# Splitting the first turned block of activations between ScalarE and VectorE, in a pooled-attention decoder trunk on Trainium2

## The chip, the cores and the metric

The kernel runs on one core of one Trainium2 chip. The metric is the device time of one execution in microseconds (us). The profile names the engines PE (TensorE matmuls), PEld (TensorE weight loads, which overlap PE), DVE (VectorE), ACT (ScalarE), POOL (GpSimd) and SP (SyncE, which here issues most of the DMAs).

## The reference, cut to what matters

Two layers work on an input `x` of 512 tokens by 1024 channels in float32. Layer 0 mixes the tokens by a causal multi-scale pooling, layer 1 by a differential attention; each is followed by a SwiGLU feed-forward network with 2816 hidden rows.

```python
for i in range(DEPTH):                                   # DEPTH = 2
    h = _multiscale_pool(x, ...) if i == 0 else _diff_attention(x, ...)
    x = _layernorm(ALPHA * x + h, ln_mix_g[i], ln_mix_b[i])
    x = _layernorm(ALPHA * x + _swiglu(x, w_gate[i], w_up[i], w_down[i]), ln_ffn_g[i], ln_ffn_b[i])
```

The change lies where layer 0 passes from the pooling mixer's layer norm (number 0) to the first gate and up products of its feed-forward network.

## The kernel before, in words

**Numbers in two parts.** Every float32 matrix product is made of three matmuls on a rounded high part and a low part (the rest): high by high, high by low, low by high (`mm3`, lines 147 to 151, so the three matmuls show as L149, L150 and L151). `split` (lines 116 to 124) makes the parts: ScalarE copies the high part (L123), then VectorE, or GpSimd where `low` says so, subtracts it from the source (L124). Weights arrive by SP's DMAs into five buffers `raw` (L111). `ready(upto)` splits the weight rows up to a number into `w<c>h` and `w<c>l`; w2 to w5 are the weights of the first gate, the first up, the second gate and the second up product.

**Tokens.** The 512 tokens are four blocks of 128. `res` holds them with tokens on the partitions. For each block s the mixer's matmuls (`mixed`, into PSUM banks `mix`) are added to `res` (`residual`, L183), the sums for mean and variance are taken (`stat`, L190), mean and variance are put together (`spread_of`, L196 to L199; the power of -0.5 runs on GpSimd, L199), and `norm` (L208) writes the normalised block. `summed` is `residual` and `stat` together.

**Turns.** The feed-forward network needs the block with channels on the partitions and in two parts, in `xt`. `transposed(0, s)` makes eight 128x128 transposes on TensorE into two PSUM banks `pt` of four each (L235). `turned(0, s)` then goes bank by bank: four ScalarE activations apply gain and bias (L249) into an SBUF tile `y`, and `split` makes `xt`'s two parts out of `y`, 512 columns at a time. Blocks 0 and 1 are turned before the feed-forward network starts; blocks 2 and 3 in its midst, at the places that the argument `late` names.

**Order.** All instructions stand in an order written by hand (`manual_schedule`): each engine runs its own in the order in which the program issues them, and waits on semaphores for the others. At the start of the network `ffn` makes three pairs of a gate and an up product (`early = 3`; f counts the pairs, i is 0 for gate and 1 for up), first for tokens 0 to 255 (`lo = 0`), then for tokens 256 to 511. A product is 24 matmuls of 256 columns: for each of the eight k blocks the three of `mm3`. Behind the product (f, i) of the first half stands `late[f, i]`, if there is one, then `advance`, which splits the next weights (g_4 and g_5, L610 and L613). `lines`, a small table for layer 1, is written to DRAM by a DMA that ScalarE issues (L487 to L491).

Of the kernel before, what the change touches and what calls it, by code (L numbers as in the profile page):

```python
# [12 lines left out]
F32 = mybir.dt.float32  # L13
F32R = mybir.dt.float32r
BF16 = mybir.dt.bfloat16
AF = mybir.ActivationFunctionType
ALU = mybir.AluOpType

P = 128
# [4 lines left out]
KB = D // P  # L24
SB = S // P
FB = FF // P
HEADS = 8
# [10 lines left out]
LINE = 640  # L38
NEAR = 512
# [15 lines left out]
def trunk(ctx, tc, x, wall, pscale, lam_p, subln, table, lng, lnb, band, first, onehot, out):  # L55
    nc = tc.nc

    keep = ctx.enter_context(tc.tile_pool(name="keep", bufs=1))
# [3 lines left out]
    def bank(name):  # L62
        return ps.tile([P, 512], F32, tag="bank", name=name)


    xt = keep.tile([P, 2, 2, KB, 256], F32R, name="xt")
# [49 lines left out]
    def split(dst_h, dst_l, src, scale=1.0, low=None):  # L116
        if scale != 1.0:
            nc.scalar.mul(dst_h, src, scale)
            nc.vector.scalar_tensor_tensor(
                dst_l, src, scale, dst_h.bitcast(F32), op0=ALU.mult, op1=ALU.subtract  # L120
            )
        else:
            nc.scalar.copy(dst_h, src)  # L123
            (low or nc.vector).tensor_tensor(dst_l, src, dst_h.bitcast(F32), op=ALU.subtract)  # L124

    def ready(upto, low=None):
        while divided[0] < min(upto, total):
            c = divided[0]
            fetch(c + RAWS)
            h, l = weight_pair(f"w{c}")  # L130
            raw = raws.pop(c)
            if c in by_dma:
                nc.scalar.copy(h, raw)
                nc.scalar.mul(l, raw, -1.0)
                nc.gpsimd.dma_start(
                    out=l, in_=wall[rows_of_wall[c]].bitcast(F32R), accum_op=ALU.add
                )
            else:
                split(h, l, raw, low=low)
            parts[c] = (h, l)  # L140
            divided[0] += 1
# [18 lines left out]
    gT = keep.tile([P, 2 * DEPTH, KB], F32, name="gT")  # L160
    bT = keep.tile([P, 2 * DEPTH, KB], F32, name="bT")

    def x_at(k, lo, hi):

        if hi - lo > 256:
            return tuple(xt[:, :, i, k, :] for i in range(2))
        a = lo // 256
        return tuple(xt[:, a, i, k, lo - 256 * a : hi - 256 * a] for i in range(2))

    def wide(acc, lo, hi):  # L170
        return acc.rearrange("p (a b) -> p a b", a=2) if hi - lo > 256 else acc[:, lo:hi]
# [9 lines left out]
    def residual(s, d, acc, scale=ALPHA):  # L181
        z = res[:, s, d * 512 : (d + 1) * 512]
        nc.vector.scalar_tensor_tensor(z, z, scale, acc, op0=ALU.mult, op1=ALU.add)  # L183
# [3 lines left out]
    def stat(n, s, d):  # L187
        if (n, s) not in stats:
            stats[n, s] = keep.tile([P, 2, 6], F32, tag="st", name=f"st{n}_{s}", bufs=4)
        nc.vector.bn_stats(stats[n, s][:, d, :], res[:, s, d * 512 : (d + 1) * 512])  # L190
# [3 lines left out]
    def spread_of(n, s):  # L194
        mv = keep.tile([P, 2], F32, tag="mv", name=f"mv{n}_{s}", bufs=2)
        nc.vector.bn_aggr(mv, stats.pop((n, s)))  # L196
        rs = keep.tile([P, 1], F32, tag="rs", name=f"rs{n}_{s}", bufs=2)
        nc.vector.tensor_scalar(rs, mv[:, 1:2], scalar1=EPS, scalar2=None, op0=ALU.add)  # L198
        nc.gpsimd.tensor_tensor(rs, rs, mhalf, op=ALU.pow)  # L199
        scales[n, s] = (mv, rs)  # L200

    def norm(n, s, done=None):
        if (n, s) not in scales:
            spread_of(n, s)
        mv, rs = scales.pop((n, s))
        z = res[:, s, :]
        if not done:
            nc.vector.tensor_scalar(  # L208
                z, z, scalar1=mv[:, 0:1], scalar2=rs, op0=ALU.subtract, op1=ALU.mult
            )  # L210
            return
        gb = gbs[n]
        halves = [slice(d * 512, (d + 1) * 512) for d in range(2)]
        for c in halves:
            nc.vector.scalar_tensor_tensor(
                z[:, c], z[:, c], mv[:, 0:1], gb[:, 0, c], op0=ALU.subtract, op1=ALU.mult
            )
        for c in halves:
            nc.vector.scalar_tensor_tensor(
                z[:, c], z[:, c], rs, gb[:, 1, c], op0=ALU.mult, op1=ALU.add  # L220
            )
            done(s, c)
# [7 lines left out]
    turns = {}  # L230
# [10 lines left out]
    def turned(n, s, kept=None):  # L241
        for i, pt in enumerate(turns.pop((n, s))):
            if kept:
                y = kept[i][:, :, s % 2 * P : (s % 2 + 1) * P]
            else:
                y = keep.tile([P, 4, P], F32, tag="y", name=f"y{n}_{s}_{i}", bufs=2)
            for k in range(4):
                kk = 4 * i + k
                nc.scalar.activation(  # L249
                    y[:, k, :],  # L250
                    pt[:, k * P : (k + 1) * P],
                    AF.Identity,
                    bias=bT[:, n, kk : kk + 1],
                    scale=gT[:, n, kk : kk + 1],
                )
            o = (s % 2) * P
            split(*(xt[:, s // 2, j, 4 * i : 4 * i + 4, o : o + P] for j in range(2)), y)

    def turn(n, s):
        transposed(n, s)  # L260
        turned(n, s)
# [21 lines left out]
    with tc.tile_pool(name="pool", bufs=1) as pp:  # L283
# [108 lines left out]
        def split_pooled(half, *groups):  # L392
            for g in groups:
                c = slice(half * 256, (half + 1) * 256)
                split(
                    ph[:, 2 * g : 2 * g + 2, c],
                    pl[:, 2 * g : 2 * g + 2, c],
                    made[half, g].rearrange("p (k t) -> p k t", k=2),
                )

        mixes = {}
# [19 lines left out]
        def summed(s, *ds):  # L421
            for d in ds:
                residual(s, d, mixes[s][d])
                stat(0, s, d)
# [25 lines left out]
        mixed(2, 0)  # L450
        summed(0, 1)
        spread_of(0, 0)
        split_pooled(1, 2, 3)
        norm(0, 0)
        tbh = pp.tile([33, HEADS], F32R, name="tbh")
        tbl = pp.tile([33, HEADS], F32R, name="tbl")
        ohr = pp.tile([33, NEAR], F32R, name="ohr")
        split(tbh, tbl, tb)
        nc.scalar.copy(ohr, oh_)
        transposed(0, 0)  # L460
# [4 lines left out]
        mm(lines_bank[:HEADS], tbl, ohr, start=False, stop=True)  # L465
        summed(1, 0, 1)
        spread_of(0, 1)
        summed(2, 0)
        norm(0, 1)
        transposed(0, 1)  # L470
        mixed(3, 1)
        turned(0, 0)
        summed(2, 1)
        spread_of(0, 2)
        turned(0, 1)
        ready(4)
        summed(3, 0, 1)
        norm(0, 2)
        spread_of(0, 3)
        ready(5)  # L480
        norm(0, 3)
        ready(6)

        line = pp.tile([HEADS, LINE], F32, name="line")
        far = pp.tile([HEADS, 1], F32, name="far")
        nc.gpsimd.memset(line[:, NEAR:], 0.0)
        nc.scalar.copy(far, lines_bank[:HEADS, NEAR - 1 :])  # L487
        nc.scalar.activation(
            line[:, :NEAR], lines_bank[:HEADS], AF.Identity, bias=far, scale=-1.0
# [14 lines left out]
    def ffn(layer, late):  # L504
        n = 2 * layer + 1
# [4 lines left out]
        with tc.tile_pool(name=f"ffn{layer}", bufs=1) as fp:  # L510
# [111 lines left out]
                if upto > len(chunks):  # L622
                    prepare(upto - len(chunks), upto - len(chunks))

            def product(acc, j, lo, hi):
                h, l = halves[j]
                for k in range(KB):
                    mm3(
                        wide(acc, lo, hi),
                        (h[:, k * P : (k + 1) * P], l[:, k * P : (k + 1) * P]),  # L630
                        x_at(k, lo, hi),
                        k == 0,
                        k == KB - 1,
                    )
# [155 lines left out]
            accs = [(bank(f"g{layer}_{f}"), bank(f"u{layer}_{f}")) for f in range(early)]  # L790
# [3 lines left out]
            for lo in (0, 256):  # L794
                for f in range(early):
                    for i in range(2):
                        product(accs[f][i], 2 * f + i, lo, lo + 256)
                        if not lo and (f, i) in late:
                            late[f, i]()
                        if not lo:  # L800
                            advance(2 * early, True)
                    if lo:
                        advance(2 * f + 6)
                        gated(order[f], *accs[f])
                        affine(n - 1, f)
                        catch_up()
                        if f < 2:
                            weight_sums()
                            next(sums)
                        if f == 1:  # L810
                            behind.append(sum_hidden(0))
# [83 lines left out]
            f = early  # L895
# [40 lines left out]
            banks = {}  # L936
            done = store if final else None
            for p in DOWN:
# [5 lines left out]
                accs = banks[{"P1": "P1", "Q5": "Q5", "Q3": "Q5", "P2": "P2"}.get(p, "P1")]  # L944
                together = len(PAIRS) - (tail if p == "Q4" else 0)
                for i in range(together):
                    j = j0 + i
# [463 lines left out]
    def later(n, s):  # L1411
        return lambda: turn(n, s)

    ffn(0, {(0, 1): later(0, 2), (1, 0): later(0, 3)})
    attention()
    ffn(1, {(0, 1): later(2, 3)})

# [107 lines left out]
```

## Time and profile before

| | |
|---|---|
| Time, median of 3 runs (lowest, highest) | 948.29 us (948.05 to 949.07) |
| Time of the profiled execution | 948.47 us |
| Its span from the first to the last instruction | 946.7 us |
| Mean granted TensorE clock | 0.997 |
| Busy: PE, PEld, DVE, ACT, POOL | 931.2, 829.9, 787.3, 513.8, 126.5 us |

The span leaves 1.8 us of the profiled execution outside the trace. A line of a timeline gives the start in us, the time of it, the engine, the line of the kernel, the operation, the tiles it writes and reads, and in brackets how long the engine had stood idle before and what ended that. Rows of one kind in a row are merged (x4). On DVE and PE the next instruction starts a little before the one ahead of it has ended, so that the distance between starts is shorter than the durations.

### The profile page before, as it was taken

The page shows a single profiled execution, that of the slowest core. Times are in us where ns is not written, and L with a number is a line of the kernel's source. Part 1 is how long each engine was busy: PE and PEld are TensorE (multiplying, and loading weights), DVE is VectorE, ACT ScalarE, POOL GpSimd, SP SyncE. Part 2 cuts the span into 40 slices and gives each one's busy share as a digit, 9 for nine tenths or more (in the row PEclk, how much of TensorE's full clock was granted, in tenths as well). Part 3 has the DMA queues.
Part 4 walks back from the last instruction along what each step waited for, and adds up shares of the span by engine and source line. Part 5 has one row for each costly group of instructions (what it writes and reads, how often), then busy time and mean ns, then how long its engine had stood idle before and what let it go on. Part 6 is the DMA issues. An engine that isn't in the chain of part 4 may idle for free.

```text
span 946.7 us, 14942 instructions
## 1 busy us (share of the span) xinstructions
PE 931.2 (98%) x5712; PEld 829.9 (88%) x5712; DVE 787.3 (83%) x1158; ACT 513.8 (54%) x819; POOL 126.5 (13%) x152
## 2 busy tenths in 40 slices
PE   9999999999999999999999999999999999999996
PEld 8898899999988878887888878998899999988884
DVE  8858989999988489968887886789779999987778
ACT  6752344555564357666878753843345554664450
POOL 4120211110001201101111100211111110001101
PEclk9999999999999999999999999999999999999998
DMA  8386988986868996875666522396988886878952
GB/s 240 125 267 225 327 265 273 269 251 215 256 209 270 350 314 189 211 196 150 155 160 138 141 90 81 118 325 214 270 252 248 251 278 202 258 248 276 349 169 90
DMA packets 86038, 211.11 MB, mean 223 GB/s; under 512 B 15140, under 2 KB 26660, under 8 KB 85966
## 3 DMA queue, kind: packets, MB, share of 16 engines
q1 hardware_dynamic: 43420, 117.16, 37.5%
q0 software_dynamic: 18768, 58.20, 24.8%
q10 hardware_dynamic: 23778, 34.78, 10.2%
q8 instruction: 45, 0.74, 0.3%
q14 instruction: 27, 0.22, 0.1%
HBM read 173.40 MB, written 36.72 MB: 222 GB/s over the span
## 4 chain that ended last, share of the span: by engine, by line
PE 82%; DVE 9%; ACT 3%; DMA 3%; issue 2%; POOL 0%; DVEq 0%; ACTq 0%; POOLq 0%
PE A L861 17%; PE P L928 9%; PE C L861 9%; PE B L861 4%; PE Q L928 3%; PE g L151 3%; PE u L149 3%; PE u L150 3%; PE u L151 3%; PE g L149 3%; PE g L150 3%; PE va L1076 2%; PE s L1142 2%; DMA r<-tsum 1%; DMA r<-in_wall 1%
## 5 line engine op out<-in xcount | busy, mean ns | idle before, releaser
L607 DVE TENSOR_TENSOR raw<-raw,raw 128x1024 f32<-128x1024 f32 x56 | 68.3, 1219 | 0.5
L123 ACT CAST xs<-hid 128x512 fp32r<-128x512 f32 (+1 forms) x60 | 34.7, 582 | 24.4 <-DVE hid L775 24.4
L124 DVE TENSOR_TENSOR xs<-hid,xs 128x512 fp32r<-128x512 f32 (+1 forms) x60 | 38.5, 643 | 7.8 <-ACT xs L123 7.8
L1158 ACT ACTIVATE p<-p,mn 128x128 f32<-128x128 f32 (+3 forms) x64 | 35.2, 552 | 12.4 <-DVE mn L1153 12.4
L249 ACT ACTIVATE y<-pt,bT,gT 128x128 f32<-128x128 f32 x80 | 30.1, 456 | 19.4 <-PE pt L235 19.4
L706 POOL DMA_DIRECT2D b<-in_wall x20 | 14.0, 706 | 170.8 <-DMA tsum<-b 70.4
L767 POOL DMA_DIRECT2D xs<-ssum x24 | 17.4, 726 | 141.6 <-PE Q L928 68.5
L199 POOL TENSOR_TENSOR rs<-rs,mhalf 128x1 f32<-128x1 f32 x16 | 12.5, 784 | 152.0 <-DVE rs L198 112.6
L639 DVE TENSOR_TENSOR hid<-sg,u 128x512 f32<-128x512 f32 x16 | 11.0, 687 | 26.1 <-PE u L151 14.1
L743 ACT CAST v<-u 128x512 fp32r<-128x512 f32 x22 | 13.6, 620 | 27.7 <-DVE u L741 27.7
L706 POOL DMA_DIRECT2D hid<-in_wall x24 | 18.7, 823 | 74.4 <-DMA tsum<-hid 43.9
L1153 DVE CUSTOM_DVE_ANT_0 p<-s,bias 128x128 f32<-128x128 f32 (+3 forms) x64 | 28.0, 485 | 0.7 <-PE s L1142 0.7
L124 DVE TENSOR_TENSOR xt<-y,xt 128x512 fp32r<-128x512 f32 x20 | 13.6, 690 | 12.1 <-ACT xt L123 12.1
L190 DVE BATCH_NORM_STATS2 st<-res 128x6 f32<-128x512 f32 x32 | 22.2, 695 | 1.1
L887 ACT ACTIVATE sg<-sg 128x512 f32<-128x512 f32 x14 | 8.9, 633 | 25.7 <-DVE sg L880 25.7
L707 POOL DMA_DIRECT2D hid<-in_wall x12 | 14.8, 1233 | 58.5 <-DMA hid<-in_wall 51.1
L655 ACT CAST xs<-hid 128x1024 fp32r<-128x1024 f32 x8 | 8.4, 1051 | 26.0 <-DVE hid L672 11.6
L1142 PE MATMUL s<-heads 64*128 64x256 f32 (+2 forms) x168 | 20.0, 353 | 1.1 <-ACT heads L123 0.8
L1142 PEld LDWEIGHTS s<-heads 64*128 64x128 f32 x168 | 14.1, 185 | 5.2 <-issue 1.0
L1172 DVE SCALAR_TENSOR_TENSOR p<-p,sm,p 128x128 f32<-128x128 f32 (+3 forms) x32 | 17.7, 552 | 1.1
L876 DVE TENSOR_TENSOR hid<-C,hid 128x512 f32<-128x512 f32 x14 | 9.7, 691 | 10.4 <-PE C L861 8.8
L872 ACT COPY hid<-C 128x512 f32<-128x512 f32 x14 | 8.2, 589 | 18.5 <-PE C L861 18.5
(1187 smaller groups left out, 3666.3 us busy)
## 6 DMA issues: line engine op xcount, KB each, us to landing
raw<-in_wall SPq DMA_DIRECT2D x122, 512.0 KB, 4.8
r<-tsum SPq DMA_DIRECT2D x40, 512.0 KB, 4.5
hid<-in_wall POOLq DMA_DIRECT2D x36, 512.0 KB, 7.4
b<-in_wall POOLq DMA_DIRECT2D x30, 512.0 KB, 6.0
r<-in_wall SPq DMA_DIRECT2D x30, 512.0 KB, 4.6
tsum<-hid ACTq DMA_DIRECT2D x24, 512.0 KB, 5.6
ssum<-v ACTq DMA_DIRECT2D x22, 512.0 KB, 4.3
tsum<-b ACTq DMA_DIRECT2D x20, 512.0 KB, 4.9
```

What stands on the lines that cost most here:

```text
L123: nc.scalar.copy(dst_h, src)
L124: (low or nc.vector).tensor_tensor(dst_l, src, dst_h.bitcast(F32), op=ALU.subtract)
L149: nc.tensor.matmul(acc, ah, bh, start=start, stop=False)
L150: nc.tensor.matmul(acc, ah, bl, start=False, stop=False)
L151: nc.tensor.matmul(acc, al, bh, start=False, stop=stop)
L249: nc.scalar.activation(y[:, k, :], pt[:, k * P : (k + 1) * P], AF.Identity, bias=bT[:, n, kk : kk + 1], scale=gT[:, n, kk : kk + 1],)
L607: tt(t, raws[pair[0]], raws[pair[1]], op=ALU.add)
L706: nc.gpsimd.dma_start(out=t[:, j], in_=src[:, j])
L861: nc.tensor.matmul(o, w[:, c], x[:, kk, :], start=p in ("P1", "Q5", "P2") and f + kk + e == 0, stop=p in ("Q4", "Q3", "P2") and (f, kk, e) ...
L928: nc.tensor.matmul(accs[s], x[:, k, r], y[:, c], start=first and k == 0 and e == 0, stop=last and k == m - 1 and e == 2, skip_group_check= ...
L1142: nc.tensor.matmul(accs[c][:, :wide], a[r, qs], b[r, :wide], start=i == 0, stop=i == 2)
L1158: nc.scalar.activation(p, p, AF.Exp, bias=mn[:, q, c : c + 1], scale=-1.0, accum_out=sm[:, q, c : c + 1],)
```

## The change

Six things are changed, all in the stretch from the mixer's end to the first half of the first three product pairs.

1. `turned(0, 1)` becomes `turned_apart(0, 1)`: ScalarE's eight activations read the PSUM banks and write the rounded high parts straight into `xt`; VectorE's eight `tensor_scalar` read the same banks and write `y`; then VectorE subtracts twice.
2. The first gate product (layer 0, f = i = 0, tokens 0 to 255) takes, for each half of the k blocks, four high by high, four low weight by high, then four high weight by low.
3. `ready(4)`, which splits w3, stands ahead of `split_pooled(1, 2, 3)` and `norm(0, 0)`, and its subtraction is on GpSimd. `ready(5)` stands behind the turn of block 1, `ready(6)` behind `spread_of(0, 2)`.
4. Of `summed(2, 0)` the `stat` is moved behind the turn and `ready(5)`; `norm(0, 2)` comes ahead of `summed(3, 0, 1)`.
5. The tiles `line` and `far` and the GpSimd memset of `line` are moved ahead, behind `norm(0, 0)`.
6. Blocks 2 and 3 are turned behind the products (1, 0) and (1, 1) instead of (0, 1) and (1, 0).

```diff
+    def turned_apart(n, s):
+        o = (s % 2) * P
+        banks = turns.pop((n, s))
+        ys = []
+        for i, pt in enumerate(banks):
+            y = keep.tile([P, 4, P], F32, tag="y", name=f"y{n}_{s}_{i}", bufs=2)
+            for k in range(4):
+                kk = 4 * i + k
+                bias, scale = bT[:, n, kk : kk + 1], gT[:, n, kk : kk + 1]
+                a = pt[:, k * P : (k + 1) * P]
+                nc.scalar.activation(
+                    xt[:, s // 2, 0, kk, o : o + P], a, AF.Identity, bias=bias, scale=scale
+                )
+                nc.vector.tensor_scalar(
+                    y[:, k, :], a, scalar1=scale, scalar2=bias, op0=ALU.mult, op1=ALU.add
+                )
+            ys.append(y)
+        for i, y in enumerate(ys):
+            h, l = (xt[:, s // 2, j, 4 * i : 4 * i + 4, o : o + P] for j in range(2))
+            nc.vector.tensor_tensor(l, y, h.bitcast(F32), op=ALU.subtract)
...
         spread_of(0, 0)
+        ready(4, nc.gpsimd)
         split_pooled(1, 2, 3)
         norm(0, 0)
...
+        line = pp.tile([HEADS, LINE], F32, name="line")
+        far = pp.tile([HEADS, 1], F32, name="far")
+        nc.gpsimd.memset(line[:, NEAR:], 0.0)
         split(tbh, tbl, tb)
...
-        summed(2, 0)
+        residual(2, 0, mixes[2][0])
         norm(0, 1)
         transposed(0, 1)
         mixed(3, 1)
         turned(0, 0)
+        turned_apart(0, 1)
+        ready(5)
+        stat(0, 2, 0)
         summed(2, 1)
         spread_of(0, 2)
-        turned(0, 1)
-        ready(4)
+        ready(6)
+        norm(0, 2)
         summed(3, 0, 1)
-        norm(0, 2)
         spread_of(0, 3)
-        ready(5)
         norm(0, 3)
-        ready(6)
...
-            def product(acc, j, lo, hi):
+            def product(acc, j, lo, hi, apart=False):
                 h, l = halves[j]
+                if apart:
+                    for b in range(2):
+                        for w, i in ((h, 0), (l, 0), (h, 1)):
+                            for k in range(4 * b, 4 * b + 4):
+                                nc.tensor.matmul(
+                                    wide(acc, lo, hi), w[:, k * P : (k + 1) * P],
+                                    x_at(k, lo, hi)[i], start=w is h and i == k == 0,
+                                    stop=(i, k) == (1, KB - 1),
+                                )
+                    return
...
-                        product(accs[f][i], 2 * f + i, lo, lo + 256)
+                        product(
+                            accs[f][i], 2 * f + i, lo, lo + 256, layer == f == i == lo == 0
+                        )
...
-    ffn(0, {(0, 1): later(0, 2), (1, 0): later(0, 3)})
+    ffn(0, {(1, 0): later(0, 2), (1, 1): later(0, 3)})
```

More of the change, by code (lines that the diff above doesn't have):

```diff
@@ L472, in trunk @@
         turned(0, 0)
+        turned_apart(0, 1)
+        ready(5)
+        stat(0, 2, 0)
         summed(2, 1)
         spread_of(0, 2)
-        turned(0, 1)
-        ready(4)
+        ready(6)
+        norm(0, 2)
         summed(3, 0, 1)
-        norm(0, 2)
         spread_of(0, 3)
-        ready(5)
         norm(0, 3)
-        ready(6)
-        line = pp.tile([HEADS, LINE], F32, name="line")
-        far = pp.tile([HEADS, 1], F32, name="far")
-        nc.gpsimd.memset(line[:, NEAR:], 0.0)
         nc.scalar.copy(far, lines_bank[:HEADS, NEAR - 1 :])
```

## The prediction

> **What bounds the kernel now.** I read the page's chain of work first, then busy time by stretch, then the timelines of PE, ACT, DVE and POOL from 15 to 54 us, since all edits lie there.
>
> ```profile
> PE 82%; DVE 9%; ACT 3%; DMA 3%; issue 2%; POOL 0%; DVEq 0%; ACTq 0%; POOLq 0%
> 52.00:70.00 18.00, 18.00 (x152) 18.00 (x152) 10.61 (x12) 8.70 (x11) 5.41 (x6) 1.00 0.82 226
> 100.00:200.00 100.00, 100.00 (x735) 95.60 (x734) 91.79 (x111) 47.54 (x61) 14.97 (x18) 1.00 0.92 285
> ```
>
> From 52 us on TensorE has no idle time in these stretches (first number the length, second PE busy), so a shift of the products there is a shift of the end. In the first row 152 matmuls of 256 columns fill 18.00 us: 0.12 us each, 24 to a product, 2.9 us a product. What the change can win or lose are TensorE's gaps ahead of 53.87 us, where the second half (tokens 256 to 511) starts:
>
> ```profile
> 24.69 1.04 PE L235 MATMUL pt<-ident,res 128*128 128x128 f32 x8
> 29.68 1.06 PE L235 MATMUL pt<-ident,res 128*128 128x128 f32 x8 [0.54 <-DVE res L208]
> 30.50 0.36 PE L149 MATMUL mix<-pw1h,pooled 128*128 128x256 f32 x1
> 32.55 0.38 PE L149 MATMUL g<-xt,w2h 128*128 128x256 f32 x1 [0.38 <-ACT xt L123]
> 33.28 0.39 PE L150 MATMUL g<-xt,w2h 128*128 128x256 f32 x1 [0.34 <-DVE xt L124]
> 35.34 0.38 PE L150 MATMUL g<-xt,w2h 128*128 128x256 f32 x1 [0.34 <-DVE xt L124]
> 36.76 0.28 PE L149 MATMUL u<-xt,w3h 128*128 128x256 f32 x1
> 40.27 1.07 PE L235 MATMUL pt<-ident,res 128*128 128x128 f32 x8 [0.47 <-DVE mv L196]
> 41.63 0.38 PE L151 MATMUL g<-xt,w4l 128*128 128x256 f32 x1
> 53.87 0.28 PE L149 MATMUL g<-xt,w2h 128*128 128x256 f32 x1
> ```
>
> The transposes of block 1 (29.68) wait for `norm(0, 1)`. The first gate product runs from 32.55 to 36.76, 4.2 us for 2.9 us of matmuls: it waits for block 1's high part, for its low part, and for the low part of the second bank (35.34). From 36.76 to 53.87 are 17.1 us, for five products (14.4) and two turns (0.8 each, as 29.68 to 30.50): 1.0 us is lost, most of it ahead of 40.27, which waits for `norm(0, 2)`. In all some 3 us can be won.
>
> **Part 1: w3 earlier.** It takes a cast and a subtraction out of the crowded stretch, but its cast now stands on ACT ahead of the casts of `split_pooled(1, 2, 3)`.
>
> ```profile
> 17.69 2.06 ACT L123 CAST pooled<-pool 128x512 fp32r<-128x512 f32 x4 [1.01 <-PE pool L390]
> 34.47 1.04 ACT L123 CAST w3h<-raw 128x1024 fp32r<-128x1024 f32 x1
> ```
> ```profile
> 15.38 2.58 SPq L111 DMA_DIRECT2D raw<-in_wall  x1
> raw<-in_wall SPq DMA_DIRECT2D x1, 512.0 KB, 6.2
> ```
> ```profile
> 22.33 1.28 DVE L124 TENSOR_TENSOR pooled<-pool,pooled 128x512 fp32r<-128x512 f32 x2
> 23.53 0.81 DVE L208 TENSOR_SCALAR res<-res,mv,rs 128x1024 f32<-128x1024 f32 x1
> 27.40 0.69 DVE L183 SCALAR_TENSOR_TENSOR res<-res,mix 128x512 f32<-128x512 f32 x1
> 28.12 0.69 DVE L190 BATCH_NORM_STATS2 st<-res 128x6 f32<-128x512 f32 x1
> 28.73 0.80 DVE L208 TENSOR_SCALAR res<-res,mv,rs 128x1024 f32<-128x1024 f32 x1
> ```
>
> w3's raw weights are the DMA issued at 15.38; it lands 6.2 us later, at 21.6. Before, the four pooled casts were done by 19.8. Now the last two wait behind w3's cast, which ends at 22.65; they end at 23.2 and 23.7. Their subtractions on DVE start at 23.2 instead of 22.33, so `norm(0, 0)` could start at 24.4 instead of 23.53: 0.9 us later. Everything behind it on DVE moves with it: the sums of block 1, block 2's residual, `norm(0, 1)`. Against that, part 4 takes the 0.7 us `stat` (28.12) from ahead of `norm(0, 1)`. Nearly nothing is left: `norm(0, 1)` starts at 29.0, and the transposes of block 1 at 30.0 instead of 29.68 (+0.3). If the weights landed early enough (by 20.7), this would be 0.6 us the other way.
>
> The subtraction of w3 is now on GpSimd, and `norm(0, 0)` meets it:
>
> ```profile
> 16.70 1.22 DVE L124 TENSOR_TENSOR pw1l<-raw,pw1h 128x1024 fp32r<-128x1024 f32 x1
> ```
> ```profile
> 16.75 3.46 POOL L124 TENSOR_TENSOR w2l<-raw,w2h 128x1024 fp32r<-128x1024 f32 x1 [0.60 <-ACT w2h L123]
> 22.56 0.55 POOL L199 TENSOR_TENSOR rs<-rs,mhalf 128x1 f32<-128x1 f32 x1 [2.34 <-DVE rs L198]
> 40.57 1.41 POOL L199 TENSOR_TENSOR rs<-rs,mhalf 128x1 f32<-128x1 f32 x1 [6.94 <-DVE rs L198]
> 447.15 1.30 POOL L124 TENSOR_TENSOR sql<-sq,sqh 128x512 fp32r<-128x512 f32 x1 [10.85 <-ACT sqh L123]
> ```
> ```profile
> 40.35 1.22 DVE L124 TENSOR_TENSOR w4l<-raw,w4h 128x1024 fp32r<-128x1024 f32 x1
> 42.02 0.82 DVE L208 TENSOR_SCALAR res<-res,mv,rs 128x1024 f32<-128x1024 f32 x1 [0.44 <-POOL rs L199]
> ```
>
> GpSimd and VectorE shut each other out here: the power on one column takes 0.55 us alone, but 1.41 when it starts inside w4's subtraction (40.35 to 41.57), and it ends 0.4 us after that. The same for w2l: 3.46 us, of which 1.17 lie inside pw1l's subtraction, so 2.3 us alone (a row of half the size takes 1.30). In the changed kernel the order is turned round: w3l starts behind the power of block 0, at 23.15, runs to 25.5, and `norm(0, 0)` comes at 24.4. No row shows a DVE operation of this kind starting inside a GpSimd subtraction. Bounds: 0 (only the later starter on GpSimd waits) to 1.1 us (DVE waits for w3l's end; a gain is excluded, nothing is removed here). I take 1.1, since the 1.41 row shows an exclusion and not a sharing. `norm(0, 0)` then starts at 25.5, the transposes of block 0 at 26.5 instead of 24.69, of block 1 at 31.1 (+1.4).
>
> The Trainium skill's "SBUF — State Buffer", section "Who interferes with whom", says the port pair that VectorE and GpSimd share is an exclusive lock held for a whole instruction, and that issue order decides who waits. By it the 1.1 us are paid; without it the sum is 1.1 us less. The 1.41 us row agrees for one order; the other no row here shows.
>
> **Part 2: the turn set apart.** It removes two ACT casts of 0.62 us and gives DVE eight `tensor_scalar`. What matters is whether both engines may read one bank at a time.
>
> ```profile
> 29.68 0.64 PE pt L235 x4
> 30.32 0.02 issue
> 30.34 1.52 ACT y L249 x4
> ```
>
> These pieces of the chain show how the program orders a bank: the first activation reads 128 columns, which the first transpose wrote, and yet is released only by the fourth, the last into this bank. Accesses of different engines are thus ordered by whole banks, not by columns. I take it that the reads of ACT and DVE are ordered the same way, in program order: activation 0, `tensor_scalar` 0, activation 1, and so on, one at a time within a bank. That costs:
>
> ```profile
> 30.34 1.51 ACT L249 ACTIVATE y<-pt,bT,gT 128x128 f32<-128x128 f32 x4 [0.80 <-PE pt L235]
> 31.88 0.62 ACT L123 CAST xt<-y 128x512 fp32r<-128x512 f32 x1
> 421.39 0.40 ACT L1158 ACTIVATE p<-p,mn 128x128 f32<-128x128 f32 x1 [1.36 <-DVE mn L1153]
> ```
> ```profile
> 32.53 0.69 DVE L124 TENSOR_TENSOR xt<-y,xt 128x512 fp32r<-128x512 f32 x1
> 35.54 1.23 DVE L124 TENSOR_TENSOR w3l<-raw,w3h 128x1024 fp32r<-128x1024 f32 x1 [0.26 <-ACT w3h L123]
> 421.05 0.29 DVE L1153 CUSTOM_DVE_ANT_0 p<-s,bias 128x128 f32<-128x128 f32 x1 [0.72 <-PE s L1142]
> L1168 DVE TENSOR_SCALAR p<-p,sm,nlam 128x128 f32<-128x128 f32 x8 | 2.8, 346 | 0.3
> ```
>
> Four overlapping activations take 1.51 us at starts 0.35 apart, so one takes 0.46. Hop from ACT to DVE 0.03 (cast ends 32.50, subtraction starts 32.53), from DVE to ACT 0.05 (421.34 to 421.39). The new `tensor_scalar` lies between 0.29 (L1153, same shape from PSUM) and 0.46 (ACT on the same shape); I take 0.35, the L1168 row, the same operation with two scalars. One round is 0.46 + 0.03 + 0.35 + 0.05 = 0.89 us (0.83 to 1.00).
>
> Without the 1.1 us of part 1: activation 0 at 30.65 (transposes at 30.0 and four of them); the fourth ends at 30.65 + 3 x 0.89 + 0.46 = 33.8; the second bank's first starts beside `tensor_scalar` 3, at 33.65, and its last `tensor_scalar` ends at about 37.15. Only then, in DVE's order, come the two subtractions (0.6 apart, 0.69 each): the first low part is there at 37.75, the second at 38.4. Before, they were there at 33.2 and 35.3. Queued on DVE behind this: w4's subtraction and block 2's sums.
>
> **Part 3: the product's order.** High by high and low weight by high of the first four k blocks, eight matmuls, are 0.95 us of cover. They end at 34.3 (gated by the fourth activation); then TensorE waits for the low part until 37.8, 3.5 us. The 16 matmuls left (1.9 us) end the product at 39.7, against 36.76: +2.95.
>
> **Parts 4 to 6, and the sum.** From there: five products and two turns, 16.1 us, if nothing is late. w3l is long done. w4's subtraction ends at 39.5, needed at 42.6. `stat`, block 2's second sum, w5's subtraction and the power follow; `norm(0, 2)` ends at about 44.2, and the transposes of block 2, moved behind (1, 0), start at 45.4. Block 3's sums and norm take 4.6 us more, to 48.8; its transposes come at 49.1. Block 3's ACT work of 4.2 us ends at 54.8, the first bank's low part is there at 53.2; the second half starts at 55.9. So the moved turns and `norm(0, 2)` hide the 1.0 us lost before, with 0.3 us to spare at block 3; without the move 40.27's wait would come back larger. The memset of `line` frees ACT earlier, where it had time anyway. SP's next weight DMA waits for w3l, 10 us earlier than before: no cost.
>
> Sum: +0.3 at the transposes and +2.65 in the turn and product make +2.95; minus 0.9 of the old waits, +2.1; with the 1.1 us of part 1, +3.2 us. On the profiled execution that is 948.47 + 3.2 = 951.7; the median of the runs is 0.2 lower, so 951.5.
>
> **The rivals.**
>
> *Norm does not wait* for GpSimd: +2.1, 950.4. For it: no row shows DVE waiting on GpSimd. Against: the 1.41 row.
>
> *Both read at once.* If reads of two engines are not ordered, activations start 0.35 apart, the high parts are there at 33.6, the `tensor_scalar` end at 33.4, the low parts at 34.0 and 34.7; the product ends at 36.0, 0.8 us earlier than before; with the 0.9 us of the old waits it is -1.7, 946.6, and 945.7 if w3's weights also land in time (the transposes at 29.1 instead of 30.0). With the 1.1 us of part 1 it is -0.6. For it: two reads change nothing in the bank. Against: the bank-wide wait above. It decides from the second activation: 0.35 us behind the first, or 0.8 and more.
>
> The Trainium skill's "PSUM — Partial Sum Buffer", section "PSUM bank collisions raise a hardware error", says that two engines on one bank at once are an error, two reads included, and to guard PSUM by bank. By it the reads alternate, and the change loses 2.1 to 3.2; without it the sum is that of this rival. The chain agrees for a write and a read; for two reads no row here does.
>
> *The dear end.* `tensor_scalar` at 0.46: seven rounds at 0.11 more, +0.8, and block 3's norm then 0.3 to 0.5 late: 952.8.
>
> **How the numbers follow.** A measurement of this kernel can tell about 0.2% (1.9 us) from no change. Alternating reads with norm waiting: 0.50, 951.5, its own range 950.6 to 952.8. Alternating, norm not waiting: 0.30, 950.4, from 949.5 (0.29 for `tensor_scalar`) to 951.2. Both read at once: 0.17, 945.7 to 947.8. Something else: 0.03. The range is 947.6 to 952.9: it leaves out the simultaneous reads without a wait of norm, and little above. Slower by over 0.2% (above 950.2): nearly all of the first case and half of the second, 0.64. Within 0.2%: the rest of the second, and half of the third, 0.24. Faster: 0.12.
>
> **What would show it.** In the changed profile: the pooled casts on ACT torn apart around a w3 cast at 21.6; `norm(0, 0)` on DVE longer than 0.8 us or starting at 25.5; L249's successor on ACT in single activations with gaps of 0.4 us, each ended by DVE, and DVE's by ACT; one TensorE wait of about 3.5 us for the low part inside the first product; no wait at the transposes of block 2. The prediction is wrong if the eight activations run in one piece within 3 us.

## The result: slower by 0.5%, and the profile after

| | before | changed |
|---|---|---|
| Time, median of 6 runs each (lowest, highest) | 948.17 us (947.55 to 949.90) | 953.48 us (952.74 to 954.88) |
| Ratio of the times, 95% interval | | 1.0054 (1.0041 to 1.0067) |
| Time of the profiled execution | 948.47 us | 953.28 us |
| Its span, mean granted clock | 946.7 us, 0.997 | 951.5 us, 0.996 |
| Start of the second half | 53.87 us | 58.70 us |

The changed kernel takes 5.3 us longer by the medians and 4.8 by the profiled executions. The forecast was 3.2 us longer, at most 4.6 by its range; the measured time lies above that range. The whole difference is made ahead of the second half, which starts 4.83 us later. The timeline of PE in the changed kernel, with the rows that answer to those of before:

```profile
26.31 1.06 PE L235 MATMUL pt<-ident,res 128*128 128x128 f32 x8 [1.79 <-DVE tbl L124]
...
30.94 1.07 PE L235 MATMUL pt<-ident,res 128*128 128x128 f32 x8 [0.15 <-DVE res L208]
...
35.16 0.64 PE L653 MATMUL g<-xt,w2l 128*128 128x256 f32 x4
39.15 2.08 PE L653 MATMUL g<-xt,w2h 128*128 128x256 f32 x8 [3.35 <-DVE xt L278]
41.02 1.05 PE L653 MATMUL g<-xt,w2l 128*128 128x256 f32 x4
41.88 0.88 PE L653 MATMUL g<-xt,w2h 128*128 128x256 f32 x4
42.59 0.28 PE L149 MATMUL u<-xt,w3h 128*128 128x256 f32 x1
...
48.34 1.04 PE L235 MATMUL pt<-ident,res 128*128 128x128 f32 x8
...
52.08 1.04 PE L235 MATMUL pt<-ident,res 128*128 128x128 f32 x8
...
58.70 0.28 PE L149 MATMUL g<-xt,w2h 128*128 128x256 f32 x1
```

Four readings. Block 1's transposes start at 30.94 instead of 29.68. Inside the first product stands one wait of 3.35 us for the low part. The 16 matmuls behind it take from 39.15 to 42.59, which is 3.44 us, or 0.215 each, where before they stood 0.12 apart. From 42.59 on nothing waits: both moved turns (48.34, 52.08) come without a bracket, and 42.59 to 58.70 are 16.1 us against 17.1 before.

Why 16 matmuls take 3.44 us, the busy time by stretch shows (length, then busy time of PE, PEld, DVE, ACT and POOL with the number of instructions, the clock that TensorE was granted, where 1.00 is full speed, DMA share, GB/s). First the changed kernel, then the kernel before:

```profile
24.00:29.00 5.00, 3.21 (x28) 3.03 (x27) 4.90 (x9) 2.56 (x7) 1.61 (x2) 1.00 0.77 292
36.50:40.00 3.50, 0.85 (x4) 0.85 (x5) 2.44 (x6) 2.84 (x5) 0.00 (x0) 0.85 0.00 0
40.00:42.00 2.00, 2.00 (x11) 2.00 (x11) 2.00 (x3) 1.54 (x2) 0.00 (x0) 0.50 0.08 14
42.00:44.00 2.00, 2.00 (x17) 2.00 (x16) 1.90 (x5) 1.14 (x2) 0.68 (x1) 0.90 0.80 307
```
```profile
36.50:40.00 3.50, 3.29 (x28) 3.09 (x26) 3.43 (x6) 1.63 (x3) 0.00 (x0) 1.00 0.42 152
```

Busy is not fast: PE is 2.00 of 2.00 us busy from 40 to 42, at half the clock, with 11 matmuls where 17 would fit at 0.12 us. The clock is 1.00 until about 39.0 and again from about 42.4, 0.50 between.

ACT's and DVE's timelines in the changed kernel, around w3's cast and in the turn:

```profile
21.93 1.05 ACT L123 CAST w3h<-raw 128x1024 fp32r<-128x1024 f32 x1 [3.49 <-DMA raw<-in_wall]
22.89 1.07 ACT L123 CAST pooled<-pool 128x512 fp32r<-128x512 f32 x2
...
31.61 0.46 ACT L269 ACTIVATE xt<-pt,bT,gT 128x128 fp32r<-128x128 f32 x1 [0.41 <-PE pt L235]
32.55 0.46 ACT L269 ACTIVATE xt<-pt,bT,gT 128x128 fp32r<-128x128 f32 x1 [0.48 <-DVE y L272]
...
37.59 0.46 ACT L269 ACTIVATE xt<-pt,bT,gT 128x128 fp32r<-128x128 f32 x1 [0.48 <-DVE y L272]
```
```profile
24.70 1.46 DVE L208 TENSOR_SCALAR res<-res,mv,rs 128x1024 f32<-128x1024 f32 x1
...
32.10 0.41 DVE L272 TENSOR_SCALAR y<-pt,gT,bT 128x128 f32<-128x128 f32 x1
33.04 0.41 DVE L272 TENSOR_SCALAR y<-pt,gT,bT 128x128 f32<-128x128 f32 x1 [0.53 <-ACT xt L269]
...
38.08 0.41 DVE L272 TENSOR_SCALAR y<-pt,gT,bT 128x128 f32<-128x128 f32 x1 [0.53 <-ACT xt L269]
38.41 1.28 DVE L278 TENSOR_TENSOR xt<-y,xt 128x512 fp32r<-128x512 f32 x2
```

Each engine is the other's releaser: activation, `tensor_scalar`, activation, in a rhythm of 0.94 us (31.61, 32.55). `norm(0, 0)` takes 1.46 us instead of 0.81. Beside it, on POOL, stands w3's subtraction:

```profile
23.09 2.41 POOL L124 TENSOR_TENSOR w3l<-raw,w3h 128x1024 fp32r<-128x1024 f32 x1
```

It ends at 25.50, `norm(0, 0)` at 26.16.

### The profile page after: what moved, and what is told of

Its sections match the earlier page's. It is cut to its first block, busy times and chain, and to the rows that moved or that the text cites. A ratio compares the mean times of both kernels' runs of the same rounds, so it can differ in the third digit from the quotient of the medians.

```text
span 951.5 us, 14946 instructions
## 1 busy us (share of the span) xinstructions
PE 931.8 (98%) x5712; PEld 830.7 (87%) x5712; DVE 790.1 (83%) x1165; ACT 514.0 (54%) x817; POOL 128.4 (13%) x153
## 4 chain that ended last, share of the span: by engine, by line
PE 78%; DVE 9%; DMA 6%; ACT 3%; issue 2%; SPq 1%; POOL 0%; DVEq 0%; ACTq 0%; POOLq 0%
PE A L895 17%; PE C L895 8%; PE P L962 6%; PE B L895 4%; PE Q L962 3%; PE u L151 3%; PE u L150 3%; PE u L149 3%; PE g L151 3%; PE g L150 3%; PE g L149 3%; DMA r<-tsum 2%; PE va L1110 2%; PE s L1176 2%; DMA r<-in_wall 2%
## 5 line engine op out<-in xcount | busy, mean ns | idle before, releaser
L249 ACT ACTIVATE y<-pt,bT,gT 128x128 f32<-128x128 f32 x72 | 27.1, 456 | 22.4 <-PE pt L235 22.3
```

## The experiments

Theory A: the loss is the turn in lockstep by bank, plus the clock that falls in TensorE's long wait, plus `norm(0, 0)` held by w3's subtraction on GpSimd; the rest of the change gives back 1 us. Its rivals (the other letters of the expectations) each put another cause in one place of it: the 3.44 us of the 16 matmuls come from something else than the wait; the late `norm(0, 0)` comes from the cast's place on ScalarE; the moved turns, the moved sums or the new order of the product cost something; the two engines are slow as a pair and not by the bank. All ratios are to the kernel before on the same chip, with 95% intervals; its median was 948.23 us in both sets (25 and 17 runs). The changed kernel, against which gains are given too, was measured in a set of its own, in which the kernel before took 948.17 us.

**1. Fill the wait.** The changed kernel, with 26 further matmuls in the place where TensorE waits. They write the half of the bank that the second half begins anew, so that the sums are not touched. All the waits of ACT and DVE stay.

```diff
             for b in range(2):
                 for w, i in ((h, 0), (l, 0), (h, 1)):
+                    if b == 0 and i == 1:
+                        for r in range(26):
+                            nc.tensor.matmul(
+                                acc[:, 256:], h[:, :P], x_at(0, lo, hi)[0],
+                                start=False, stop=False, skip_group_check=True,
+                            )
```

> The changed kernel with 26 extra matmuls in the first gate product, put where TensorE waits for the first low part (35.5 to 39.15 us in its profile); they write into columns of the bank that are begun anew later. Theory A (the wait of 3.35 us itself makes the granted clock fall, so that the next 16 matmuls stand 0.23 us apart): with the wait filled the clock stays at 1.00 in 36.5 to 40 us, the 16 matmuls take 1.9 instead of 3.4 us, the time falls by about 1.5 us against the changed kernel, to 951.9. Rival B (the slow stretch comes from the order of the product, or from what the others do meanwhile): they stay 0.23 apart and the time stays at 953.4 or rises.

Measured: 951.03 us (950.33 to 951.92), ratio 1.0025 (1.0016 to 1.0034): 2.45 us faster than the changed kernel, by work added. Its timeline of PE and its stretch:

```profile
35.31 3.28 PE L654 MATMUL g<-xt,w2h 128*128 128x256 f32 x26
38.82 1.22 PE L659 MATMUL g<-xt,w2h 128*128 128x256 f32 x8 [0.23 <-DVE xt L278]
...
40.84 0.28 PE L149 MATMUL u<-xt,w3h 128*128 128x256 f32 x1
```
```profile
36.50:40.00 3.50, 3.27 (x28) 3.07 (x26) 2.65 (x5) 2.99 (x6) 0.00 (x0) 1.00 0.00 0
```

The low part comes when it came (38.82 against 39.15; the turn began 0.3 earlier in this execution). The same 16 matmuls now take 2.02 us instead of 3.44, at a clock of 1.00. So the wait cost its own length and 1.4 us more, and this is the part without a term in the prediction. The gain by the medians is 1 us larger than that. Of the changed kernel's six executions five show a mean clock of 0.993 or 0.994 and only the profiled one 0.996, while those of this one show 0.996 to 0.998; a longer low stretch in most executions would explain it. No trace of those five was taken, but experiment 5 has one at 0.993, and there the stretch is twice as long. It is not shown, because the five are hardly slower than the profiled one (median 953.54 us against 953.28). Between the two profiled executions 1.72 us of the difference lie ahead of the second half (it starts at 56.98 against 58.70). The other 1.0 us lies behind that, where the nine profiled kernels scatter by 1.4 us (from the start of the second half to the end of the span 891.8 to 893.2 us).

**2. The plain turn back.** `turned(0, 1)` again; all else stays.

```diff
-        turned_apart(0, 1)
+        turned(0, 1)
```

> The changed kernel with block 1 turned as before (activations into y, cast, subtraction), all else kept. Theory A (the alternating reads are the main cost): the low part of the first bank is there at 34.4 instead of 39.15, no wait over 1 us, no fall of the clock; the first product ends at about 37.3 instead of 42.6, some 0.7 us may be lost at the transposes of block 3; in all 948.5, about the kernel before. Rival C (the early w3 is the main cost): it stays 3 us and more above the kernel before.

Measured: 948.63 us (947.36 to 949.94), ratio 1.0000 (0.9992 to 1.0009). All the other parts together come to nothing that can be measured, and the 4.9 us to the changed kernel are the turn's. In DVE's timeline of this kernel `norm(0, 0)` is still held, by w3's subtraction, which runs from 23.33 to 25.75:

```profile
24.34 1.96 DVE L208 TENSOR_SCALAR res<-res,mv,rs 128x1024 f32<-128x1024 f32 x1
```

The first product ends at 37.54, and block 3's transposes now wait 0.47 us for its norm (47.68).

**3. w3 late, on VectorE.** The changed kernel with `ready(4)` behind the turn.

```diff
         spread_of(0, 0)
-        ready(4, nc.gpsimd)
         split_pooled(1, 2, 3)
...
         turned_apart(0, 1)
+        ready(4)
         ready(5)
```

> The changed kernel with w3 prepared late: cast and VectorE subtraction of w3 stand behind the turn of block 1, ahead of w4. Theory A: norm of block 0 is back at 23.5 us and the transposes of block 1 come at 29.1 instead of 30.9; the alternation and the fall of the clock stay; about 1.8 us below the changed kernel, 951.6. Rival C: it gains 4 us or more, down to the kernel before.

Measured: 951.79 us (950.60 to 952.58), ratio 1.0031 (1.0020 to 1.0042): 1.7 us faster than the changed kernel. The timelines of PE and DVE:

```profile
29.10 1.06 PE L235 MATMUL pt<-ident,res 128*128 128x128 f32 x8
...
37.30 2.07 PE L653 MATMUL g<-xt,w2h 128*128 128x256 f32 x8 [3.35 <-DVE xt L278]
```
```profile
23.53 0.81 DVE L208 TENSOR_SCALAR res<-res,mv,rs 128x1024 f32<-128x1024 f32 x1
```

`norm(0, 0)` is back at 23.53 and 0.81 us, block 1's transposes start 1.84 us earlier than in the changed kernel (29.10), and the long wait is the same to the digit.

**4. The turn alone.** The kernel before with nothing but `turned_apart(0, 1)`: no new order of the product, no moved turn.

```diff
-        turned(0, 1)
+        turned_apart(0, 1)
```

> The kernel before with only the turn of block 1 set apart. Theory A: the reads alternate here too, and VectorE, which has block 2's sums ahead of them, starts at 32.5; the low part comes at 39.5 instead of 33.2, and TensorE, which in the old order can do one matmul only, stands still for 7 us, then runs at the low clock for some 3.4 us; 6 us slower than the kernel before, 954.3. Rival C: within 1 us of the kernel before.

Measured: 954.32 us (953.80 to 958.55), ratio 1.0066 (1.0048 to 1.0085): 6.1 us slower. The other parts of the change, which do nothing beside the plain turn, win back some 0.8 us beside the split one (954.32 to 953.48). Its PE has a longer wait, since the old order of the product has almost no cover and VectorE does block 2's sums ahead of the turn (its first `tensor_scalar` starts at 32.53, the activation's at 30.43), and the clock stays low longer:

```profile
39.57 0.58 PE L150 MATMUL g<-xt,w2h 128*128 128x256 f32 x1 [7.21 <-DVE xt L278]
```
```profile
36.50:40.00 3.50, 0.43 (x2) 0.43 (x3) 2.31 (x5) 2.54 (x5) 0.00 (x0) 0.57 0.00 0
40.00:42.00 2.00, 2.00 (x11) 2.00 (x11) 1.97 (x4) 1.97 (x4) 0.00 (x0) 0.50 0.00 0
42.00:44.00 2.00, 2.00 (x12) 2.00 (x11) 1.97 (x4) 0.06 (x1) 0.00 (x0) 0.55 0.78 225
```

**5. w3's cast behind the pooled casts.** The changed kernel with the early `ready(4)` one line down. ScalarE no longer holds the pooled casts for w3's raw weights; the subtraction stays on GpSimd, ahead of `norm(0, 0)`.

```diff
-        ready(4, nc.gpsimd)
         split_pooled(1, 2, 3)
+        ready(4, nc.gpsimd)
         norm(0, 0)
```

> The changed kernel with ready(4) one line lower, behind split_pooled(1, 2, 3), so that the pooled casts no longer wait for w3's raw weights; w3's subtraction on GpSimd still starts at 23.1 us, ahead of norm of block 0. Theory A with the lock (VectorE's norm can't run beside GpSimd's subtraction and waits for its end at 25.5): norm starts at 23.5 but ends at 26.1 as in the changed kernel, and the time stays at 953.4. Rival D (the wait for the raw weights is the whole cost of this part, the lock costs nothing): norm takes 0.8 us again, block 1's transposes come 1.3 us earlier, 952.0.

Measured: 953.45 us (952.77 to 955.90), ratio 1.0060 (1.0047 to 1.0072): no gain. DVE, POOL and the stretches of this kernel:

```profile
24.12 2.52 DVE L208 TENSOR_SCALAR res<-res,mv,rs 128x1024 f32<-128x1024 f32 x1
```
```profile
23.68 2.41 POOL L124 TENSOR_TENSOR w3l<-raw,w3h 128x1024 fp32r<-128x1024 f32 x1
```
```profile
36.50:40.00 3.50, 0.38 (x2) 0.39 (x2) 2.27 (x5) 2.54 (x5) 0.00 (x0) 0.76 0.01 2
40.00:42.00 2.00, 2.00 (x11) 2.00 (x11) 2.00 (x4) 1.53 (x4) 0.00 (x0) 0.50 0.00 0
42.00:44.00 2.00, 2.00 (x11) 2.00 (x11) 1.90 (x5) 1.57 (x2) 0.21 (x1) 0.50 0.82 272
44.00:46.00 2.00, 2.00 (x15) 2.00 (x14) 1.56 (x3) 0.00 (x0) 1.21 (x1) 0.72 1.04 412
```

In this execution the work ahead ran later (GpSimd's power of block 0 starts at 23.16 instead of 22.56). Even so `norm(0, 0)` starts 0.58 us earlier than in the changed kernel, and it takes 1.06 longer. It ends at 26.64, 0.55 behind the end of w3's subtraction (26.09); in the changed kernel the distance was 0.66, in experiment 2 0.55 (26.30 against 25.75). In the changed kernel GpSimd's memset of `line` still came in between (25.42 to 25.62), and the norm ended 0.54 behind that. The end of GpSimd's instruction sets the end of the norm, whatever its start: an exclusion, not a sharing, and the place of the cast does not matter as long as the subtraction goes ahead.

The stretches show something else. TensorE's wait is again 3.35 us (up to 39.62), but the clock is low for 6.8 us, from 38.3 to 45.1, where it was 3.4 in the changed kernel. Slow are here not only the 16 matmuls behind the wait but 9 more: 25 matmuls from 39.62 to 45.12, 5.5 us where 3.0 would do. The same wait cost 1.5 us of clock in one execution and 2.5 in the other.

**6. Crossed banks.** The changed kernel, but ScalarE reads bank 0 while VectorE reads bank 1, and then the other way round. The instructions are the same, eight and eight.

```diff
...
         for i in range(2):
             for k in range(4):
-                kk = 4 * i + k
-                ...
-                nc.scalar.activation(...)          # bank i
-                nc.vector.tensor_scalar(...)       # bank i
+                kk, a, bias, scale = args(i, k)
+                nc.scalar.activation(...)          # bank i
+            for k in range(4):
+                kk, a, bias, scale = args(1 - i, k)
+                nc.vector.tensor_scalar(...)       # bank 1 - i
```

> The changed kernel with the reads of the two banks crossed: while ScalarE reads the first bank, VectorE reads the second, then they change over, so that the engines hand over once per bank instead of after each read. Theory A (ordering by bank is what makes the reads alternate): four activations in a run of 1.5 us, four tensor_scalar in a run of 1.5 us, the first low part at 35.5 instead of 39.15, the first product's end at 37.5 instead of 42.6, clock at 1.00, in all 948.3. Rival E (the two engines' PSUM reads hinder each other in whatever bank): no better than 951.

Measured: 947.92 us (947.14 to 948.54), ratio 0.9996 (0.9987 to 1.0005): 5.6 us faster than the changed kernel. Timelines of ACT, DVE and PE:

```profile
31.84 1.50 ACT L273 ACTIVATE xt<-pt,bT,gT 128x128 fp32r<-128x128 f32 x4 [0.41 <-PE pt L235]
33.69 1.50 ACT L273 ACTIVATE xt<-pt,bT,gT 128x128 fp32r<-128x128 f32 x4 [0.34 <-DVE y L278]
```
```profile
32.28 2.64 DVE L278 TENSOR_SCALAR y<-pt,gT,bT 128x128 f32<-128x128 f32 x8
```
```profile
35.70 1.22 PE L658 MATMUL g<-xt,w2h 128*128 128x256 f32 x8 [1.07 <-DVE xt L283]
```

The two engines are not slow as a pair: four activations are merged in 1.50 us again, and eight `tensor_scalar` take 2.64 us. ACT hands over to DVE once for each bank and not once for each 128 columns. The long wait is 1.07 us.

**7. Everything mended.** Crossed banks; w3's subtraction on GpSimd behind `norm(0, 0)`, held there by a product on one column that reads the norm's result; the low parts last over both banks in the first product; and block 3's sums in a new order. The crossing is that of experiment 6 and not printed again.

```diff
-        ready(4, nc.gpsimd)
         split_pooled(1, 2, 3)
         norm(0, 0)
+        token = pp.tile([P, 1], F32, name="token")
+        nc.gpsimd.tensor_tensor(token, res[:, 0, 0:1], mhalf, op=ALU.mult)
+        ready(4, nc.gpsimd)
...
         spread_of(0, 2)
-        ready(6)
+        summed(3, 0)
         norm(0, 2)
-        summed(3, 0, 1)
+        ready(6)
+        summed(3, 1)
...
-                    for b in range(2):
-                        for w, i in ((h, 0), (l, 0), (h, 1)):
+                    for ts in (((h, 0), (l, 0)), ((h, 1),)):
+                        for b, (w, i) in [(b, t) for b in range(2) for t in ts]:
```

> The crossed kernel with three more changes: w3 is prepared behind norm of block 0 (a one-column GpSimd product of norm's output keeps GpSimd's subtraction behind it); the first product takes high by high and low weight by high of all eight k blocks first, then high weight by low; half of block 3's sums stand ahead of norm of block 2, whose power then costs no wait. Theory A: block 1's transposes at 29.1, the first product's end at 34.7 (36.76 in the kernel before), the second half at 50.9 instead of 53.87; 945.3, 0.3% below the kernel before. If another wait comes in (block 3's transposes are the nearest), 946 to 947.

Measured: 945.29 us (944.44 to 946.39), ratio 0.9971 (0.9960 to 0.9982): 2.9 us faster than the kernel before. PE, POOL and the stretches of this kernel:

```profile
29.31 1.06 PE L235 MATMUL pt<-ident,res 128*128 128x128 f32 x8
...
34.06 1.11 PE L661 MATMUL g<-xt,w2h 128*128 128x256 f32 x8
...
51.15 0.28 PE L149 MATMUL g<-xt,w2h 128*128 128x256 f32 x1
```
```profile
24.61 0.19 POOL L482 TENSOR_TENSOR token<-res,mhalf 128x1 f32<-128x1 f32 x1 [1.30 <-DVE tbl L124]
24.76 2.42 POOL L124 TENSOR_TENSOR w3l<-raw,w3h 128x1024 fp32r<-128x1024 f32 x1
```
```profile
28.00:36.50 8.50, 8.50 (x66) 7.58 (x65) 8.39 (x17) 7.45 (x18) 0.31 (x1) 1.00 0.17 65
```

The low parts' matmuls (34.06) have no bracket, PE is busy for all of 28.0 to 36.5, and the second half starts at 51.15 instead of 53.87. Of the some 3 us that could be won by the gaps of before, 2.7 are won. How much each of the three mends brings beside the crossed banks was not tried one by one.

## Why the prediction was right in direction and short in size

**Alternation by banks (right).** Reads of ACT and DVE alternate within a bank; experiment 6 shows that it is the bank and not the pair of engines. The rival of simultaneous reads is refuted by the 0.94 us rhythm.

**The round (a little short).** It was put at 0.89 us with 0.35 for `tensor_scalar`; it measures 0.94 with 0.41. Over seven rounds that is 0.35 us. The row taken for it (L1168) reads SBUF; the new one reads PSUM, and inside the bounds that were given (0.29 to 0.46) it lies nearer to the upper. The dear end, at 0.46, did not come, though its 952.8 us is near the measured time. In the eight merged ones of experiment 6 the starts lie 0.32 apart ((2.64 - 0.41) / 7): in a row each hides part of the next, in the lockstep each is paid whole.

**The norm held by GpSimd (right).** Predicted: block 1's transposes at 31.1 with the hold; measured 30.94. The raw weights landed at 21.9 and not at 21.6, the pooled casts waited for them as described, and the norm ended at 26.16 where 26.3 was expected. It did not start late, as the text had it as one of two forms, but ran long. Experiment 3 gives the price of w3's new place, 1.84 us at the transposes; the `stat` that was moved hides 0.6 of it (29.68 to 29.10, predicted 0.7), so that 1.26 show.

**The moved turns, and the old waits (right).** No wait at 48.34 and 52.08, and 16.1 us from the end of the first product to the second half, as put down. At block 3 there was nearly nothing to spare without the late product: `norm(0, 3)` ends at 50.19, and its transposes would have been due at 50.29 if the product had ended at 40.8. In experiment 2 they do wait.

**The step that failed: the first product.** "The 16 matmuls left (1.9 us) end the product at 39.7" (40.8 with the norm held) counted the long wait at its own length and took the matmuls behind it at 0.12 us. The wait was sized right, 3.35 us against 3.5. But the clock fell in it, the 16 matmuls took 3.44 us, and the product ended at 42.59. The 1.79 us between that and 40.8 are 1.52 of clock (3.44 - 1.92), 0.35 of the rounds, less 0.16 because the transposes came early; that leaves 0.08. Together: 1.26 at the transposes and 4.57 in the turn and product are 5.83 (36.76 to 42.59), less 1.0 of old waits (0.9 in the forecast's sum), 4.83. With the clock's 1.5 in the sum the forecast would have been 953.0 us; with the 2.5 of experiment 5's trace, 954.0.

The price of this term was not in the trace of before, whose longest wait in this stretch, 0.54 us, leaves the clock at 1.00. But the trace does show that the clock falls: its last matmul ends at 937.7 us, and from about 941.4 to the end of the span the granted clock is 0.50. The Trainium skill has a rule for it in "TensorE: Matmul & The Clock Gate", section "What's actually happening": half the clock after an idle window of about 3.4 us, which runs free of the kernel, and full clock after as long a busy one. The traces here agree on the length: the low stretch lasts 3.4 us in the changed kernel (39.0 to 42.4) and twice that in experiment 4 (37.0 to 43.8, by the clock of its stretches: 3.0 us at half of 36.5 to 40, all of the next 2, and 1.8 of the last) and in experiment 5. On the idle window they do not agree in full: in experiment 5 the last matmul ahead of the wait ended at 36.27 and the clock fell at 38.3, so that the 3.4 us ahead of the fall still hold 0.9 us of matmuls. The 1.79 us wait at block 0's transposes leaves the clock at 1.00.

## What to carry to other kernels

A wait on TensorE has two prices, its length and the slow matmuls behind it. In these traces waits of up to 1.79 us left the clock alone and waits of 3.35 us and more lowered it; what lies between was not measured. A gap that is stretched that far must be charged with both, and busy time alone does not show the second: read the granted clock in the stretch behind each long wait. Two engines that shared out the elements of one PSUM bank gained nothing here and paid a hand-over for each piece; let each have a bank of its own and swap. Before a VectorE instruction is left beside a long GpSimd one, ask which comes first, and where it matters give the later one a data dependency that puts it behind.

## What the runs showed of the hardware

- The fall of the clock is not tied to the length of the wait alone. The last matmul ahead of the wait ended at 35.80 in the changed kernel, and the clock fell at about 39.0, 3.2 us later; in experiment 4 the wait of 7.21 us began at 32.36 and the clock fell at 37.0, 4.6 us later; in experiment 5, 2.0 us later. When it falls matters: in the changed kernel it fell 0.2 us ahead of the next matmul (39.15), and 3.4 us later it was back; in experiment 5 it fell 1.3 us ahead (39.62) and came back only after 6.8 us. A wait of 3.35 us thus cost 1.5 or 2.5 us in matmuls, and 26 matmuls of no use in its place took the loss away.
- VectorE's `tensor_scalar` is held by a GpSimd instruction that is already running: the norm of 0.81 us took 1.46, 1.96 and 2.52 us and ended 0.54 or 0.55 us behind the end of the GpSimd instruction that went ahead of it. Before, only the other direction could be seen.
- Behind a one-column GpSimd instruction that waits for a norm, the same GpSimd subtraction (2.42 us) runs beside VectorE's sums, which take 0.67 to 0.70 us there as elsewhere, and holds no norm: block 1's transposes start at 29.31, where with w3 out of the way they start at 29.10.
